# Relu and row sum on one core: a first load of 15 rows at a 60 KB pitch and a second of one row per partition

## The chip, the core and the metric

The kernel runs on one core of a Trainium2 chip. The metric is the device time in microseconds (us) of one execution; the kernel before takes 160.94 us, the median of three runs (160.9 to 161.1). The profile shows one further execution of it, taken by the hardware profiler, with a span of 159.6 us from its first instruction to its last.

## What is computed

`x` has 32 x 512 rows of 1024 float32 numbers, 64 MiB in all. Negative numbers count as zero, and each row is summed:

```python
def reference(x):
    relu_x = np.maximum(x, 0)
    return np.sum(relu_x, axis=-1).astype(np.float32)   # 16384 sums
```

So 67.1 MB are read once from HBM and 64 KB are written.

## The kernel before

**Tiling.** The 16384 rows are dealt to 128 partitions, 128 rows to each. A row is 4 KB. The first load brings rows 0 to 2047: partition p gets 16 consecutive rows, so that partitions lie 64 KB apart in HBM (`xf`, the pitch is 64 KB) and the whole load is one stretch of 8 MB. All later loads read from the other 14336 rows (`xv`), of which partition p owns 112 consecutive ones, so that the pitch is 448 KB; each full load takes 16 rows (64 KB) of every partition. There are seven full loads of 8 MB (`NB`, the list `TWO` has an entry for each), then a tail: a load of 8 rows, one of 4, and the last four rows of each partition in four loads of 9312, 5136, 960 and 976 bytes a partition. Full loads go around three buffers (`NBUF = 3`).

**Order.** Everything is written out by hand, with semaphores. SP issues every load and store, in program order, on one queue. The first load is moved ahead of the opening barrier (`EARLY = 1`). Loads 0 to 2 are issued at once. Load j from 3 on waits (in `load`, line 99) until DVE has finished with the buffer of load j - 3 (`freed`). The stores come last in SP's program (`store`, lines 109 and 110): the 16 sums of the first load, then 110 sums per partition, then the last two. The last instruction waits for all stores.

**Work on a load.** For most rows ACT clamps a group of rows in place (`clamp`, line 117) and DVE sums the group along the row (`total`, line 125). `TWO` gives the groups: `[16]` for loads 0 to 2, then `[8, 8]`, `[8, 8]`, `[7, 7]`. Single rows are done by one engine alone, clamp and sum in one instruction: `act_row` (line 132) on ACT, `dve_row` (line 140) on DVE. The seventh load, the tail and the last pieces are done in this way. The final sum, of the piece of 244 columns and three part sums, is line 224 on DVE.

Of the kernel before, what the change touches and what calls it, by code (L numbers as in the profile page):

```python
# [4 lines left out]
F32 = mybir.dt.float32  # L5
RELU = mybir.ActivationFunctionType.Relu
MAX, ADD = mybir.AluOpType.max, mybir.AluOpType.add
P = 128

ROWS = 16  # L10
NBUF = 3


TWO = [[16], [16], [16], [8, 8], [8, 8], [7, 7], []]
ACT = [0, 0, 0, 0, 0, 2, 9]
DVE = [0, 0, 0, 0, 0, 0, 7]

# [2 lines left out]
TAIL = [8, 4]  # L20
START_PIECE, END_PIECE = 280, 260
PIECES = [240, 244]
# [4 lines left out]
def kernel(tc: tile.TileContext, x: bass.AP, out: bass.AP):  # L27
    nc = tc.nc
    sems = Semaphores(tc)

    tc.close()
    tc.compile()
    nc.cur_bb = nc.bb_map[tc.start_bb_name]
    body = nc.cur_bb.bb.instructions
    ends = list(body)
    body.clear()
    n_stores = relu_sum(nc, sems, x, out)
    body.extend(ends)


    nc.cur_bb = nc.bb_map[tc.start_bb_name + "_end"]
    nc.cur_bb.bb.instructions.clear()
    nums = sorted(s.num for s in (*sems.loads, sems.act, sems.dve))
    cleared = range(nums[0], nums[-1] + 1)
    assert len(cleared) == len(nums)
    nc.sync.sem_clear(cleared)
    nc.sync.wait_ge(sems.stored, 16 * n_stores).then_inc(sems.stored, -16 * n_stores)
    open_without_barrier(tc, EARLY)


class Semaphores:
    def __init__(self, tc: tile.TileContext):
        n = len(TWO) + len(TAIL) + 2 + len(PIECES)
        self.loads = [tc.alloc_semaphore(f"load{i}") for i in range(n)]
        self.act = tc.alloc_semaphore("act")
        self.dve = tc.alloc_semaphore("dve")
        self.stored = tc.alloc_semaphore("stored")


def relu_sum(nc, sems: Semaphores, x: bass.AP, out: bass.AP):  # L60
    x_flat = x.flatten_outer_dims()
    N, D = x_flat.shape
    NT = N // P
    NB = len(TWO)
    assert N == P * NT == P * ROWS * (NB + 1)
# [3 lines left out]
    res = nc.alloc_sbuf_tensor("res", [P, NT], F32)  # L69
# [5 lines left out]
    ]  # L75


    N1 = P * ROWS
    xf = x_flat[:N1].rearrange("(p m) d -> p m d", p=P)
    xv = x_flat[N1:].rearrange("(p m) d -> p m d", p=P)  # L80
    o_flat = out.rearrange("b s -> (b s)")
    of = o_flat[:N1].rearrange("(p m) -> p m", p=P)
    ov = o_flat[N1:].rearrange("(p m) -> p m", p=P)

    def rows(m, n):
        if m < ROWS:
            return xf[:, m : m + n, :]
        return xv[:, m - ROWS : m - ROWS + n, :]

    def sums(m, n):  # L90
        if m < ROWS:
            return of[:, m : m + n], res[:, m : m + n]
        return ov[:, m - ROWS : m - ROWS + n], res[:, m : m + n]

    n_load = n_act = n_dve = n_store = 0
# [1 line left out]
    def load(dst, src, after=None):  # L97
        nonlocal n_load
        dma = nc.sync.dma_start(out=dst, in_=src)  # L99
        if after:  # L100
            dma.wait_op(sems.dve, after[1], "sem-ge")
        dma.then_inc(sems.loads[n_load], 16)
        n_load += 1
        return sems.loads[n_load - 1]

    def store(m, n, act, dve):
        nonlocal n_store
        dst, src = sums(m, n)
        nc.sync.wait_ge(sems.act, act)
        nc.sync.dma_start(out=dst, in_=src).wait_op(sems.dve, dve, "sem-ge").then_inc(  # L110
            sems.stored, 16
        )
        n_store += 1

    def clamp(ap, loaded):
        nonlocal n_act
        i = nc.scalar.activation(out=ap, in_=ap, func=RELU)  # L117
        if loaded is not None:
            i.wait_op(loaded, 16, "sem-ge")
        i.then_inc(sems.act, 1)  # L120
        n_act += 1

    def total(ap, m, n):
        nonlocal n_dve
        nc.vector.tensor_reduce(  # L125
            out=res[:, m : m + n], in_=ap, axis=mybir.AxisListType.X, op=ADD
        ).wait_op(sems.act, n_act, "sem-ge").then_inc(sems.dve, 1)
        n_dve += 1

    def act_row(ap, accum_out, loaded):  # L130
        nonlocal n_act
        i = nc.scalar.activation(out=ap, in_=ap, func=RELU, accum_out=accum_out)  # L132
        if loaded is not None:
            i.wait_op(loaded, 16, "sem-ge")
        i.then_inc(sems.act, 1)
        n_act += 1

    def dve_row(ap, accum_out, loaded):
        nonlocal n_dve
        i = nc.vector.tensor_scalar(  # L140
            out=ap,
            in0=ap,
            scalar1=0.0,
            scalar2=None,
            op0=MAX,
            op1=ADD,
            accum_out=accum_out,
        )
        if loaded is not None:
            i.wait_op(loaded, 16, "sem-ge")  # L150
        i.then_inc(sems.dve, 1)
        n_dve += 1

    freed = []
    m = 0
    for j in range(NB):
        buf = bufs[j % NBUF]
        loaded = load(buf[:, :, :], rows(m, ROWS), j >= NBUF and freed[j - NBUF])
        c = 0
        act_waits = dve_waits = loaded  # L160
        for n in TWO[j]:
            clamp(buf[:, c : c + n, :], act_waits)
            total(buf[:, c : c + n, :], m + c, n)
            act_waits = None
            c += n
        for _ in range(ACT[j]):
            act_row(buf[:, c, :], res[:, m + c : m + c + 1], act_waits)
            act_waits = None
            c += 1
        for _ in range(DVE[j]):  # L170
            dve_row(buf[:, c, :], res[:, m + c : m + c + 1], dve_waits)
            dve_waits = None
            c += 1
        assert c == ROWS
        freed.append((n_act, n_dve))
        m += ROWS


    buf = bufs[NB % NBUF]
    c = 0  # L180
    for n in TAIL:
        loaded = load(
            buf[:, c : c + n, :], rows(m, n), None if c else freed[NB - NBUF]
        )
        for i in range(n):
            if i % 2 == 0 or (n == 8 and i == 7):
                act_row(buf[:, c, :], res[:, m : m + 1], loaded if i == 0 else None)
            else:
                dve_row(buf[:, c, :], res[:, m : m + 1], loaded if i == 1 else None)
            c += 1  # L190
            m += 1

    flat = buf[:, :, :].rearrange("p c d -> p (c d)")
    src = rows(m, 4).rearrange("p c d -> p (c d)")
    at = c * D
    split = 2 * D
    b = split + START_PIECE
# [3 lines left out]
    loaded = load(flat[:, at : at + b], src[:, :b])  # L201
# [5 lines left out]
    loaded = load(flat[:, at + end : at + 4 * D], src[:, end:])  # L207
# [7 lines left out]

    store(0, ROWS, *freed[0])
    store(ROWS, NT - ROWS - 2, sums_act, sums_dve)

    for i in range(len(PIECES) - 1):
# [10 lines left out]
    ).wait_op(sems.dve, n_dve, "sem-ge").then_inc(sems.dve, 1)  # L232
    n_dve += 1
    store(NT - 2, 2, n_act, n_dve)
    return n_store

# [48 lines left out]
```

## Time and profile before

| what | value |
|---|---|
| time, median of 3 runs | 160.94 us (160.9 to 161.1) |
| span of the profiled execution | 159.6 us |
| difference, which lies around the span | 1.3 us |
| DVE busy | 117.6 us, 74% |
| ACT busy | 104.2 us, 65% |
| DMA queue, share of 16 engines | 98.0% |
| HBM read, mean rate over the span | 67.11 MB, 421 GB/s |
| instructions | 120 |

The page gives the profiled execution's own time as its span alone, 159.6 us; the runs' times are 1.3 us above it. Starts of instructions are counted from the start of the span. A DMA's own movement is no instruction: what is listed for SP is the issue, some 0.33 to 0.46 us each, and the landing comes later. The trace also records every DMA packet, one for each partition of a load or store, with start, duration and size.

### The profile page before, as it was taken

The numbers are of one execution on the slowest core, as the hardware profiler recorded it, in microseconds if no ns is written. First come the engines' busy times: TensorE is split into PE (matmuls) and PEld (weight loads), VectorE is DVE, ScalarE is ACT, GpSimd is POOL, SyncE is SP. The second block draws the span as 40 slices with busy tenths as digits, with TensorE's granted clock in tenths as the row PEclk, the third lists the DMA queues.
The fourth block names the chain that finished last, engine by engine and source line by source line (L and its number), as shares of the span: only waits on it lengthen the run. The fifth ranks groups of instructions, "written<-read, shape, count | busy, mean of one in ns | idle before, by whom it ended". The sixth has DMA issues, their size and how long they took to land.

```text
span 159.6 us, 120 instructions
## 1 busy us (share of the span) xinstructions
DVE 117.6 (74%) x43; ACT 104.2 (65%) x50; POOL 0.2 (0%) x4
## 2 busy tenths in 40 slices
DVE  0000000009999499994999999999999999999986
ACT  3000059990699708996099951999329993499995
POOL 0000000000000000000000000000000000000000
DMA  7996996996997999979979969969969969798993
GB/s 279 509 526 263 526 526 263 526 509 279 526 476 312 526 394 394 526 345 443 526 328 460 526 263 526 526 263 526 509 279 526 493 296 526 337 452 382 418 412 119
DMA packets 2304, 67.18 MB, mean 421 GB/s; under 512 B 640, under 2 KB 896, under 8 KB 1024
## 3 DMA queue, kind: packets, MB, share of 16 engines
q1 hardware_dynamic: 2304, 67.18, 98.0%
HBM read 67.11 MB, written 0.07 MB: 421 GB/s over the span
## 4 chain that ended last, share of the span: by engine, by line
DMA 43%; DVE 34%; ACT 17%; another core or an unknown queue 3%; SPq 1%; issue 0%
DMA io<-in_x_dram 43%; DVE res L125 32%; ACT io L117 17%; DVE io L140 1%; SPq L99 1%; DVE piece L224 0%; DVE piece L140 0%
## 5 line engine op out<-in xcount | busy, mean ns | idle before, releaser
L125 DVE TENSOR_REDUCE res<-io 128x8 f32<-128x8192 f32 (+2 forms) x9 | 101.1, 11287 | 40.0 <-ACT io L117 40.0
L117 ACT ACTIVATE io<-io 128x8192 f32<-128x8192 f32 (+2 forms) x9 | 81.7, 9110 | 47.7 <-DMA io<-in_x_dram 47.7
L132 ACT ACTIVATE io<-io 128x1024 f32<-128x1024 f32 x20 | 20.9, 1045 | 6.0 <-DMA io<-in_x_dram 6.0
L140 DVE TENSOR_SCALAR_CACHE_REDUCE io<-io 128x1024 f32<-128x1024 f32 (+2 forms) x15 | 15.8, 1110 | 0.5 <-DMA io<-in_x_dram 0.4
L132 ACT ACTIVATION_READ_ACCUMULATOR io<-io 128x1 f32 x20 | 3.8, 188 | 0.0
L117 ACT ACT_TABLE_LOAD x1 | 1.3, 1283 | 0.1
L140 DVE DVE_READ_ACCUMULATOR io<-io 128x1 f32 x15 | 1.2, 82 | 0.0
L224 DVE TENSOR_SCALAR_CACHE_REDUCE piece<-piece 128x247 f32<-128x247 f32 x1 | 0.4, 410 | 0.0
L140 DVE TENSOR_SCALAR_CACHE_REDUCE piece<-piece 128x240 f32<-128x240 f32 x1 | 0.4, 397 | 0.0
L269 POOL MEMSET const-bfloat16-1.0<- 128x1 bf16 x1 | 0.1, 101 | 0.0
L269 POOL MEMSET const-uint8-127<- 128x1 uint8 x1 | 0.1, 101 | 0.0
L269 POOL MEMSET const-float32-0.0<- 128x1 f32 x1 | 0.1, 98 | 0.2 <-issue 0.2
L269 POOL MEMSET const-float32-1.0<- 128x1 f32 x1 | 0.1, 98 | 0.0
L224 DVE DVE_READ_ACCUMULATOR piece<-piece 128x1 f32 x1 | 0.1, 83 | 0.0
L140 DVE DVE_READ_ACCUMULATOR piece<-piece 128x1 f32 x1 | 0.1, 82 | 0.0
## 6 DMA issues: line engine op xcount, KB each, us to landing
io<-in_x_dram SPq DMA_DIRECT2D x1, 4096.0 KB, 21.6
io<-in_x_dram SPq DMA_DIRECT2D x1, 2048.0 KB, 26.1
io<-in_x_dram SPq DMA_DIRECT2D x1, 1164.0 KB, 28.4
io<-in_x_dram SPq DMA_DIRECT2D x1, 642.0 KB, 29.5
piece<-in_x_dram SPq DMA_DIRECT2D x1, 122.0 KB, 29.2
piece<-in_x_dram SPq DMA_DIRECT2D x1, 120.0 KB, 29.4
io<-in_x_dram SPq DMA_DIRECT2D x7, 26.9
out_dram<-res SPq DMA_DIRECT2D x1, 55.0 KB, 1.6
```

The lines of the kernel that those rows point to most:

```text
L99: dma = nc.sync.dma_start(out=dst, in_=src)
L117: i = nc.scalar.activation(out=ap, in_=ap, func=RELU)
L125: nc.vector.tensor_reduce(out=res[:, m : m + n], in_=ap, axis=mybir.AxisListType.X, op=ADD).wait_op(sems.act, n_act, "sem-ge").then_inc(se ...
L132: i = nc.scalar.activation(out=ap, in_=ap, func=RELU, accum_out=accum_out)
L140: i = nc.vector.tensor_scalar(out=ap, in0=ap, scalar1=0.0, scalar2=None, op0=MAX, op1=ADD, accum_out=accum_out,)
L224: nc.vector.tensor_scalar(out=last[:, :], in0=last[:, :], scalar1=0.0, scalar2=None, op0=MAX, op1=ADD, accum_out=res[:, NT - 2 : NT - 1],) ...
L269: nc = _bacc.Bacc("TRN2", target_bir_lowering=False, num_devices=1)
```

## The change

The first load takes 15 rows for each partition, from rows 128 to 2047, so that partitions lie 60 KB apart. A second load brings rows 0 to 127, one stretch of 512 KB, one row (4 KB) for each partition, into the place left free in the same buffer. Only the first of the two stands ahead of the opening barrier. The single row of each partition is clamped and summed by DVE (`dve_row`) into a column of a new tile `one`, which DVE clears first and then transposes in blocks of 32 x 32 into `turned`; four partitions of `turned` then hold the 128 sums as 32 numbers each. The store of the first load's sums becomes three: the 15 sums (60 bytes) of the even partitions, those of the odd ones, and four stretches of 128 bytes from `turned`. The other two stores are as they were.

```diff
-TWO = [[16], [16], [16], [8, 8], [8, 8], [7, 7], []]
+TWO = [[15], [16], [16], [8, 8], [8, 8], [7, 7], []]
...
+    one = nc.alloc_sbuf_tensor("one", [P, 32], F32)
+    turned = nc.alloc_sbuf_tensor("turned", [P, 32], F32)
     N1 = P * ROWS
-    xf = x_flat[:N1].rearrange("(p m) d -> p m d", p=P)
+    xf = x_flat[P:N1].rearrange("(p m) d -> p m d", p=P)
...
-    of = o_flat[:N1].rearrange("(p m) -> p m", p=P)
+    oo = o_flat[:P].rearrange("(b i) -> b i", i=32)
+    of = o_flat[P:N1].rearrange("(p m) -> p m", p=P)
...
-        loaded = load(buf[:, :, :], rows(m, ROWS), j >= NBUF and freed[j - NBUF])
-        c = 0
+        c = 1 if j == 0 else 0
+        loaded = load(
+            buf[:, c:, :], rows(m + c, ROWS - c), j >= NBUF and freed[j - NBUF]
+        )
+        if j == 0:
+            ahead = load(buf[:, 0, :], x_flat[:P])
+        if j == 0:
+            nc.vector.memset(one[:, :], 0.0).then_inc(sems.dve, 1)
+            n_dve += 1
+            nc.vector.wait_ge(sems.dve, n_dve)
+            dve_row(buf[:, 0, :], one[:, 0:1], ahead)
+            nc.vector.transpose(turned[:, :], one[:, :]).wait_op(
+                sems.dve, n_dve, "sem-ge"
+            ).then_inc(sems.dve, 1)
+            n_dve += 1
+            sums_ahead = n_act, n_dve
...
-    store(0, ROWS, *freed[0])
+    store(1, ROWS - 1, *freed[0], slice(0, P, 2))
+    store(1, ROWS - 1, *freed[0], slice(1, P, 2))
+    store(0, 1, *sums_ahead)
     store(ROWS, NT - ROWS - 2, sums_act, sums_dve)
```

More of the change, by code (lines that the diff above doesn't have):

```diff
@@ L52, in __init__ @@
     def __init__(self, tc: tile.TileContext):
-        n = len(TWO) + len(TAIL) + 2 + len(PIECES)
+        n = 1 + len(TWO) + len(TAIL) + 2 + len(PIECES)
         self.loads = [tc.alloc_semaphore(f"load{i}") for i in range(n)]
@@ L86, in rows, with sums @@
         if m < ROWS:
-            return xf[:, m : m + n, :]
+            return xf[:, m - 1 : m - 1 + n, :]
         return xv[:, m - ROWS : m - ROWS + n, :]
-    def sums(m, n):
+    def sums(m, n, part):
         if m < ROWS:
-            return of[:, m : m + n], res[:, m : m + n]
+            return of[part, m - 1 : m - 1 + n], res[part, m : m + n]
         return ov[:, m - ROWS : m - ROWS + n], res[:, m : m + n]
@@ L104, in load, with store @@
         return sems.loads[n_load - 1]
-    def store(m, n, act, dve):
+    def store(m, n, act, dve, part=slice(None)):
         nonlocal n_store
-        dst, src = sums(m, n)
-        nc.sync.wait_ge(sems.act, act)
+        dst, src = (oo, turned[0::32, :]) if m == 0 else sums(m, n, part)
+        if act:
+            nc.sync.wait_ge(sems.act, act)
         nc.sync.dma_start(out=dst, in_=src).wait_op(sems.dve, dve, "sem-ge").then_inc(
```

## The prediction

> **What bounds the kernel.** I read the page's chain first, then the timeline, then busy time by stage, then the end. The chain:
>
> ```profile
> ## 4 chain that ended last, share of the span: by engine, by line
> DMA 43%; DVE 34%; ACT 17%; another core or an unknown queue 3%; SPq 1%; issue 0%
> ```
>
> It changes between engines, which hides what holds the pace. The timeline (start, duration, engine, line; in brackets the idle time before and what ended it) shows it:
>
> ```profile
> 21.87 13.86 ACT L117 ACTIVATE io<-io 128x16384 f32<-128x16384 f32 x1 [20.47 <-DMA io<-in_x_dram]
> ...
> 41.19 13.86 ACT L117 ACTIVATE io<-io 128x16384 f32<-128x16384 f32 x1 [5.46 <-DMA io<-in_x_dram]
> ...
> 60.55 13.86 ACT L117 ACTIVATE io<-io 128x16384 f32<-128x16384 f32 x1 [5.50 <-DMA io<-in_x_dram]
> 74.44 66.64 DVE L125 TENSOR_REDUCE res<-io 128x16 f32<-128x16384 f32 x7 [2.14 <-ACT io L117]
> 79.90 13.95 ACT L117 ACTIVATE io<-io 128x8192 f32<-128x8192 f32 x2 [5.50 <-DMA io<-in_x_dram]
> ```
>
> Each clamp starts as its load lands: 21.87, 41.19, 60.55, 79.90, that is 19.35 us apart, while ACT needs 13.9 and DVE 17.2. Loads set the pace. From 74.44 DVE works without a gap, through the seven totals and into the tail, but that run starts with the third load's clamp, so it moves with the loads. By stage (us, then DVE, ACT, POOL, clock, DMA share, GB/s):
>
> ```profile
> 41.20:60.50 19.30, 17.20 (x2) 13.85 (x1) 0.00 (x0) 1.00 1.00 435
> 60.50:79.90 19.40, 17.26 (x2) 13.86 (x1) 0.00 (x0) 1.00 1.00 432
> ```
>
> The DMA engines are full. The end, from the timeline:
>
> ```profile
> 155.37 1.22 DVE L140 TENSOR_SCALAR_CACHE_REDUCE io<-io 128x1024 f32<-128x1024 f32 x1 [0.43 <-DMA io<-in_x_dram]
> ...
> 157.74 0.41 DVE L224 TENSOR_SCALAR_CACHE_REDUCE piece<-piece 128x247 f32<-128x247 f32 x1
> ```
>
> DVE waits 0.43 us for the 9312-byte load, then works to 158.16; the last store follows and the span ends at 159.6. So a shift of the load stream before the third load moves DVE's run, the tail and the end alike, one for one, in both directions.
>
> **Where the stream loses time.** Only at its start. The first load needs 21.87 us where a load in the stream needs 19.35: 2.52 us. By the packet records the first packet starts 1.01 after the issue, the last packet of the load ends at 21.50, and its semaphore is complete at 21.85. What is left is 2.52 - 1.01 - 0.37 = 1.14 us: the ramp. The 16 engines' first packets start from 1.01 to 1.81, and last 2.50 to 3.27 us where all later 64 KB packets of this load last 2.418. The mean excess is 0.6, and by packet end less 2.418 the slowest engine is in step only at 2.17 (= 1.01 + 1.14, give or take 0.02). Its lag stays to the end: landings of a load are spread over 0.56 to 0.59 us throughout, and a load counts as landed with its slowest engine.
>
> **The change part by part.**
>
> *Packets.* Bytes stay the same; each engine gets 8 packets of 60 KB and 8 of 4 KB for 8 of 64 KB. Durations by size are 1.213 us (32 KB), 0.612 (16 KB), 0.199 (5136 B), 0.011 (64 B): a line with 0.0113 us for a packet. Eight more: +0.09 us. One more semaphore write of 0.009: +0.01. All of it is in the stream, on the path.
>
> *Issues.* Each load issued into the running stream (at 53.0, 72.3, 91.7, 108.9) stretched the packets in flight from 2.418 to about 2.43: 0.011. Six issues between 126.9 and 129.3 stretched theirs to 2.474, about 0.01 each. The change issues one load and two stores more: +0.03. Before any gain that is +0.13 us.
>
> [...]
>
> *The ramp.* What the new pitch does to it no row shows. Lower end: it goes to nothing, -1.14. If only the excess goes and the engines' starts stay, the slowest is in step at its start, 1.81 for 2.17: -0.36. For a shorter spread of starts speaks the last store, whose 16 engines begin within some 0.04 us (159.01 to 159.04). Upper end: a longer ramp, priced below. At 64 KB pitch the engines' first addresses are whole multiples of 64 KB apart and all read the same offset at once; at 60 KB these offsets differ. I take -0.57, half of the ramp, between the two rows: the excess is a thing of simultaneous starts (the engine starting at 1.81 has 0.08 of it, the one at 1.05 has 0.85), and the spread should shrink partly with it. Sum: -0.57 + 0.13 = -0.44 us.
>
> [...]
>
> *First buffer.* ACT clamps 15 rows in 15/16 of 13.86 = 13.0 us, from about 20.6 (without a gain) to 33.6, and DVE totals them in 16.1 to 49.7, where it was 52.98. The fourth load is then issued 3.2 us earlier, behind a queue filled to 60.2: worth nothing. Before this DVE has a memset, a row (1.21 + 0.08) and a transpose (no row; 0 to 0.41, the 247-column instruction) at about 22 to 24, queued ahead of the first total, which waits for ACT until 33.6: hidden by some 10 us; uncovered they would cost 1.8 us.
>
> *Stores.* The two added issues (0.36 us each) stand in SP's program behind the last load, at about 129.3, and SP has nothing to do until 156.5: hidden. Their packets queue behind the pieces. Before, eight 64 B packets an engine ended at 157.18 and the 110-sum store began at 157.46; eight of 60 B, one more semaphore, and on four engines a 128 B packet with one more, cost 0.01 to 0.04 by the 64 B row and 0.14 by the 440 B row (0.0257 each): under the 0.28 of cover, and the last store comes only at 159.0. Store traffic stretched some 976 B packets from 0.045 to 0.051-0.061; the last piece landed at 157.60 and DVE came to it at 157.72, cover 0.1. I take zero, and up to +0.05.
>
> **The rivals.**
>
> *The ramp has nothing to do with the pitch.* A cold path that any first packet meets gives no gain, and the sum is +0.13: 161.07 us. For it: later packets of engines that start within 2 ns of each other (4.276, 4.278, 4.282) last 2.418, at the same 64 KB multiples. Against: an engine's excess depends on who else starts.
>
> *The ramp is moved.* Engines that leave the second load in step meet the same multiples at the 448 KB pitch and pay there: also about 161.07. Against: the 448 KB load follows from the first one now without one slow packet.
>
> *Slower: the ramp is made by issues.* Three loads are issued in the first 1.33 us, and their descriptors fall into the ramp; the change puts a fourth among them. A third of 1.14 is +0.38, with 0.13 +0.51: 161.45 us. It decides from +0.19 us on, where the sum passes +0.32. For it: the ramp ends about when the third load's issue, 0.9 to 1.33, has had 1.0 us to reach the engines. Against: six issues in a row near 128 cost 0.055 together. A 4 KB phase slower than the line (0.20 us a packet for 0.16) would cost about as much.
>
> **How the numbers follow.** The time is the median plus the change of the span: 160.94 - 0.44 = 160.50. A measurement of this kernel can tell about 0.2%, 0.32 us. A shorter ramp: 0.55, from 159.93 (-1.14 + 0.13) to 160.94; 0.46 of it beyond 0.32, which asks for a ramp shorter by 0.45, and 0.09 within. Ramp independent of the pitch: 0.13; moved: 0.07; both within. Longer: 0.25, slower. The rest of uncertainty of this kind I put at 0.02, from within to slower. So 0.46, 0.27, 0.27. The range leaves out the last tenth on each side: 160.05 to 161.40; the likeliest case's own is 160.05 to 160.75.
>
> **What would show it.** Right: first packets of 60 KB near 2.27 us and starts within less than 0.8 us; the first clamp at about 20.1 (eight packets shorter by 0.15, and the 0.57); the second at 41.19 + 0.11 - 0.57 = 40.73, all later ones 0.46 earlier; 4 KB packets at 0.16; DVE's run from 73.98. Wrong: a second clamp at 41.3 (no gain) or 41.6 (issues); slow packets in the first 448 KB load (moved); 4 KB packets over 0.18; or a tail in which DVE waits for the pieces.

## The result, and the profile after

The changed kernel takes 161.56 us, the median of five runs (161.52 to 161.60), beside 161.03 for the kernel before (160.90 to 161.16): a ratio of 1.0032, 95% interval 1.0021 to 1.0043. It is slower by 0.53 us, where 0.44 faster was forecast. The profiled execution has a span of 160.1 us, 0.49 more than before.

The chain of the changed kernel has the same links in nearly the same shares, so it does not tell where 0.5 us went:

```profile
## 4 chain that ended last, share of the span: by engine, by line
DMA 44%; DVE 33%; ACT 17%; another core or an unknown queue 3%; SPq 1%; issue 0%
```

Its timeline tells (start, duration, engine, line; in brackets the idle time before and what ended it):

```profile
21.04 13.00 ACT L121 ACTIVATE io<-io 128x15360 f32<-128x15360 f32 x1 [19.64 <-DMA io<-in_x_dram]
22.29 1.22 DVE L144 TENSOR_SCALAR_CACHE_REDUCE io<-io 128x1024 f32<-128x1024 f32 x1 [22.05 <-DMA io<-in_x_dram]
...
23.55 0.21 DVE L173 STREAM_TRANSPOSE turned<-one 128x32 f32<-128x32 f32 x1
34.07 16.15 DVE L129 TENSOR_REDUCE res<-io 128x15 f32<-128x15360 f32 x1 [10.31 <-ACT io L121]
41.64 13.86 ACT L121 ACTIVATE io<-io 128x16384 f32<-128x16384 f32 x1 [7.60 <-DMA io<-in_x_dram]
...
60.99 13.86 ACT L121 ACTIVATE io<-io 128x16384 f32<-128x16384 f32 x1 [5.50 <-DMA io<-in_x_dram]
74.88 66.65 DVE L129 TENSOR_REDUCE res<-io 128x16 f32<-128x16384 f32 x7 [2.13 <-ACT io L121]
```

The second clamp starts at 41.64, before at 41.19: 0.45 us are lost by then. After that nothing is lost: the third clamp is 0.44 late, DVE's long run 0.44. The added row, the transpose (0.21 us) and the total of 15 rows lie far ahead of their turn. By stage the stream is full as before (columns as in the prediction):

```profile
41.20:60.50 19.30, 14.00 (x2) 13.86 (x1) 0.00 (x0) 1.00 1.00 435
60.50:79.90 19.40, 17.27 (x2) 13.86 (x1) 0.00 (x0) 1.00 1.01 436
```

And the end, again from the timeline, is the same picture 0.44 to 0.48 us later:

```profile
155.81 1.22 DVE L144 TENSOR_SCALAR_CACHE_REDUCE io<-io 128x1024 f32<-128x1024 f32 x1 [0.44 <-DMA io<-in_x_dram]
...
158.22 0.41 DVE L244 TENSOR_SCALAR_CACHE_REDUCE piece<-piece 128x247 f32<-128x247 f32 x1
```

So the loss is in the start of the stream. The packet records split it. I call an engine "in step" at the end of its first packet less the duration that packets of this size have later (2.418 us for 64 KB, 2.268 for 60 KB). Before, the 16 engines are in step at 1.83 us on average, the slowest at 2.17; after, at 1.95 and 2.52. The slowest has lost 0.35. The rest of the 0.45 is 0.07 for packets (8 x (2.268 + 0.159) for 8 x 2.418) and small change. The engines also keep their distance from each other: landings of one load are spread over 0.56 to 0.59 us before and 0.87 to 0.89 us after, the second load as the eighth. The pitch was to bring the engines together at the start; it drove them apart.

### The profile page after: what moved, and what is told of

Its sections match the earlier page's. It is cut to its first block, busy times and chain, and to the rows that moved or that the text cites. A ratio compares the mean times of both kernels' runs of the same rounds, so it can differ in the third digit from the quotient of the medians.

```text
span 160.1 us, 129 instructions
## 1 busy us (share of the span) xinstructions
DVE 118.1 (74%) x47; ACT 103.4 (65%) x50; POOL 0.2 (0%) x4
## 4 chain that ended last, share of the span: by engine, by line
DMA 44%; DVE 33%; ACT 17%; another core or an unknown queue 3%; SPq 1%; issue 0%
DMA io<-in_x_dram 44%; DVE res L129 32%; ACT io L121 17%; SPq L102 1%; DVE io L144 0%; DVE piece L244 0%; DVE piece L144 0%
## 5 line engine op out<-in xcount | busy, mean ns | idle before, releaser
L129 DVE TENSOR_REDUCE res<-io 128x8 f32<-128x8192 f32 (+3 forms) x9 | 100.0, 11170 | 17.7 <-ACT io L121 17.7
L121 ACT ACTIVATE io<-io 128x8192 f32<-128x8192 f32 (+3 forms) x9 | 80.9, 9015 | 49.0 <-DMA io<-in_x_dram 49.0
L144 DVE TENSOR_SCALAR_CACHE_REDUCE io<-io 128x1024 f32<-128x1024 f32 (+2 forms) x16 | 17.1, 1121 | 22.6 <-DMA io<-in_x_dram 22.5
```

The costliest lines, as they stand in the source:

```text
L129: nc.vector.tensor_reduce(out=res[:, m : m + n], in_=ap, axis=mybir.AxisListType.X, op=ADD).wait_op(sems.act, n_act, "sem-ge").then_inc(se ...
L144: i = nc.vector.tensor_scalar(out=ap, in0=ap, scalar1=0.0, scalar2=None, op0=MAX, op1=ADD, accum_out=accum_out,)
```

## The experiments

Three theories stood after this. **Issues**, the slower rival of the prediction: a fourth DMA issued within the first 2 us lengthens the ramp. **Pitch**: reading at 60 KB itself puts the slowest engine later. A third was that the ramp is a cold path that neither touches. Each comparison has its own runs of the kernel before on its chip, with a median of 161.04 to 161.09 us.

**1. The split without the pitch.**

```diff
-TWO = [[16], ...
+TWO = [[15], ...
...
+        c = 1 if j == 0 else 0
+        loaded = load(buf[:, c:, :], rows(m + c, ROWS - c), ...)
+        if j == 0:
+            ahead = load(buf[:, 0:1, :], rows(0, 1))      # xf as before: pitch 64 KB
+            dve_row(buf[:, 0, :], res[:, 0:1], ahead)
```

> The kernel before with only its first load split at the old pitch of 64 KB: 15 rows per partition, then the one row left, which DVE clamps and sums; stores as before. So it has the fourth early issue without the new pitch and without the new stores. Theory of the issues (a fourth issue within the first 2 us makes the ramp longer): the ramp grows by about the 0.35 us that the slowest engine lost in the changed kernel, 0.09 for packets and semaphores, together +0.45 us, second clamp at about 41.6. Theory of the pitch (60 KB itself puts the slowest engine later): +0.1 us, second clamp at 41.3.

Measured: 161.22 beside 161.09, ratio 1.0008 (0.9999 to 1.0016), +0.13 us. Slowest engine in step at 2.25, landings of a full load spread over 0.52 to 0.57 us. The clamp of the first 448 KB load in this kernel:

```profile
41.42 13.86 ACT L117 ACTIVATE io<-io 128x16384 f32<-128x16384 f32 x1 [7.57 <-DMA io<-in_x_dram]
```

That is between the two expectations, 41.3 and 41.6, but the time agrees with the price of packets and issue alone (+0.1), not with +0.45. A fourth early issue with packets of 60 KB does not make the loss: the interval, -0.02 to +0.26 us, holds the 0.1 and not the 0.45.

**2. The pitch without the fourth early issue.** The changed kernel with the single row loaded later, into a tile of its own.

```diff
-        if j == 0:
-            ahead = load(buf[:, 0, :], x_flat[:P])
+        if j == 2:
+            nc.sync.wait_ge(sems.act, 1)
+            ahead = load(alone[:, :], x_flat[:P])
...
```

> The changed kernel with its single-row load taken out of the start: issued only after the first clamp, into a tile of its own, summed by DVE between the second and the third total. The first load keeps 15 rows at 60 KB; three issues stand in the first 1.4 us as in the kernel before. Theory of the issues: the slowest engine is in step at about 2.17 us as before, what is left is packets and stores, +0.1 to +0.15 us against the kernel before. Theory of the pitch: the slowest engine is in step at about 2.5 us, +0.45 to +0.5 us.

Measured: 161.39 beside 161.09, ratio 1.0017 (1.0008 to 1.0026), +0.30 us; slowest engine in step at 2.44. The ramp is that of the theory of the pitch (2.5 expected) though only three loads are issued early; the time is below its +0.45.

**3. The kernel before with one issue in the ramp.**

```diff
+    nc.vector.memset(bufs[2][:, 0:8, :], 0.0).then_inc(sems.dve, 1)
+    n_dve += 1
...
+        if j == 1:
+            nc.sync.wait_ge(sems.dve, 1)
```

> The kernel before, with loads 1 and 2 issued only when a DVE memset of a free buffer is over (some us after the start, still long before the first load has landed). One issue is left in the ramp. Theory of the issues: each of the three costs about 0.35 us of the ramp of 1.14, so two fewer give -0.7 us, and first packets start closer together than 0.8 us and last less than 2.6. Theory of the pitch, and that of a cold path: 0, first packets as before, slowest engine in step at 2.17.

Measured: 161.09 beside 161.09, ratio 0.9997 (0.9989 to 1.0006). Loads 1 and 2 were issued at 8.77 and 9.14 us, the memset being over at 8.73:

```profile
1.85 6.88 DVE L156 MEMSET io<- 128x8192 f32 x1 [1.85 <-issue]
21.88 13.86 ACT L117 ACTIVATE io<-io 128x16384 f32<-128x16384 f32 x1 [20.48 <-DMA io<-in_x_dram]
```

The first clamp starts at 21.88 all the same (21.87 before), and the slowest engine is in step at 2.18. At 64 KB the ramp does not depend on the issues behind it: -0.7 was expected of the theory of the issues, 0 came.

**4. The changed kernel with one issue in the ramp**, the same edit in the changed kernel, ahead of its second load.

> The changed kernel with the same delay ahead of its second load: 60 KB pitch, one issue in the ramp. Theory of the issues: ramp as in the delayed kernel before, so about -0.7 from the ramp, +0.1 for packets, +0.05 for the tail: -0.55 us against the kernel before. Theory of the pitch: as the changed kernel, +0.5. A cold path: the ramp of before, +0.15.

Measured: 161.50 beside 161.09, ratio 1.0019 (1.0011 to 1.0028); slowest engine in step at 2.42. Again no gain of the kind that issues would give. Whether 0.41 is less than the 0.53 of the changed kernel, this run can't say, since the two were not measured side by side; in numbers 13 and 14 they are.

**5 to 8. The pitch alone.** One number changed in the kernel before, nothing else: same instructions, same packets of 64 KB, same stores.

```diff
-    xf = x_flat[:N1].rearrange("(p m) d -> p m d", p=P)
+    xf = bass.AP(x_flat.tensor, x_flat.offset, [[PITCH * D, P], [D, ROWS], [1, D]])
```

> The kernel before with one number changed: the first load still takes 16 rows (64 KB) of every partition in one DMA, but from addresses 60 KB apart, so that one row in 16 is read twice and the sums of the first load are of other rows than the reference's. No split, no new instruction, stores as before. Theory of the pitch: 60 KB alone makes the engines leave the ramp further apart, landings spread over 0.85 to 1.0 us instead of 0.56, the slowest in step at 2.42 to 2.52 instead of 2.17, +0.25 to +0.35 us. Rival (the split or the smaller packet does it, the split load at 64 KB was a lucky one): spread 0.56, time within 0.1 us of the kernel before.

> As the kernel with the 60 KB pitch alone, but at 68 KB (17 rows): again the sums of the first load are of other rows. If any pitch that is no multiple of 64 KB spreads the engines, this gives +0.25 to +0.35 us too, with landings 0.85 to 1.0 us apart; if 60 KB is special, or the partitions' overlap in reads is what matters (none here), it gives the time of the kernel before.

> As above at 512 KB (128 rows), a multiple of 64 KB and a large power of two; the sums of the first load are of other rows. If multiples of 64 KB are what keeps the engines together: spread 0.5 to 0.6 us, time within 0.1 us of the kernel before. [...]

> As above at 32 KB (8 rows, so that neighbouring partitions read half of their rows twice; the sums of the first load are of other rows). Half of the partitions are multiples of 64 KB apart. Theory of the multiples of 64 KB: between the two, spread 0.6 to 0.85 us, +0.1 to +0.2 us; if it is a matter of smaller pitches than 64 KB: as the 60 KB one or worse.

Measured: 60 KB 161.37 (ratio 1.0016, 1.0007 to 1.0025), 68 KB 161.62 (1.0035, 1.0021 to 1.0048), 512 KB 161.43 (1.0026, 1.0016 to 1.0037), 32 KB 161.00 (0.9997, 0.9988 to 1.0006), all beside 161.09. Here are the first two clamps at 60 KB, then at 68 KB:

```profile
22.08 13.86 ACT L118 ACTIVATE io<-io 128x16384 f32<-128x16384 f32 x1 [20.67 <-DMA io<-in_x_dram]
41.42 13.86 ACT L118 ACTIVATE io<-io 128x16384 f32<-128x16384 f32 x1 [5.49 <-DMA io<-in_x_dram]
```

```profile
22.47 13.86 ACT L118 ACTIVATE io<-io 128x16384 f32<-128x16384 f32 x1 [21.07 <-DMA io<-in_x_dram]
41.79 13.86 ACT L118 ACTIVATE io<-io 128x16384 f32<-128x16384 f32 x1 [5.46 <-DMA io<-in_x_dram]
```

The first clamp comes 0.21 and 0.60 us later than before, the second 0.23 and 0.60: what is lost in the first packets stays lost, nothing is added. The pitch alone does it, in one DMA, without a split. That 512 KB costs about as much, and 32 KB nothing, was not what the theory of multiples of 64 KB expected. The Trainium skill's page "DMA: Bandwidth & Descriptors", section "Latency and other measured facts", has 207 GB/s per direction at a row pitch of 512 KiB, for copies between HBM tensors in tiles of 128 partitions x 16 KiB, and calls 214 the full rate; by that row 512 KiB costs next to nothing. This case agrees: with 64 KB per partition the median packet of the 512 KB load lasts 2.420 us, at 64 KB 2.418, and only the ramp is longer.

**9 and 10. The stores.** The changed kernel again, and without its three early stores.

```diff
-    store(1, ROWS - 1, *freed[0], slice(0, P, 2))
-    store(1, ROWS - 1, *freed[0], slice(1, P, 2))
-    store(0, 1, *sums_ahead)
```

> The changed kernel unchanged, beside the next one on the same chip. If pitch and split are all there is: +0.39 us (0.26 of the 60 KB pitch alone and 0.13 of the split alone), slowest engine in step at 2.4 to 2.5. If the fourth early issue or the stores add something: about +0.53 as first measured.

> The changed kernel without its three early stores (the sums of rows 0 to 2047 are not written). If the stores cost nothing on the path, as forecast: the time of the changed kernel to within 0.05 us. If three early stores for one cost the 0.05 to 0.14 us that the parts leave over: the changed kernel less about 0.1.

Measured: 161.59 and 161.59 beside 161.04, ratios 1.0032 (1.0020 to 1.0045) and 1.0031 (1.0019 to 1.0042). No cost of the stores shows; with intervals of some 0.2 us to each side, 0.1 us would not show. The changed kernel's loss repeats, +0.55.

**11 and 12. More pitches**, the one-number edit again.

> The kernel before with the first load's addresses 16 KB apart (4 rows; neighbouring partitions read three quarters of their rows twice, and the sums of the first load are of other rows). If it matters that the first packets of the engines lie at multiples of 64 KB from each other (an engine has 8 partitions, so that 16 engines' first partitions lie at least 4 apart): landings spread 0.5 to 0.6 us, time as the kernel before within 0.1 us. If the smaller pitch or the smaller stretch of memory shortens the ramp: -0.1 to -0.4 us.

> The same at 128 KB (32 rows; the sums of the first load are of other rows). If multiples of 64 KB keep the engines together and 512 KB is a case of its own: time of the kernel before within 0.1 us, spread 0.5 to 0.6. If the stretch of memory is what spreads them (8 MB at 64 KB, 16 MB here, 64 MB at 512 KB, where +0.42 was measured): +0.1 to +0.3 us, engines starting later as at 512 KB.

Measured beside 161.04: 16 KB 161.38 (ratio 1.0020, 1.0011 to 1.0029), 128 KB 161.01 (0.9998, 0.9989 to 1.0007). The expectation that 16 KB would cost nothing missed; so did the one that a longer stretch of memory is what counts.

**13 and 14. What is left over.** The changed kernel and its delayed form on one chip.

> The changed kernel once more, beside its delayed form on the same chip. Pitch alone gave +0.26 us and the split alone +0.13; the changed kernel gave +0.53 and +0.55. If the fourth issue within the ramp costs something at this pitch: +0.5 us here, and 0.1 to 0.15 less in the delayed form; the fourth issue lasts 0.77 us or more here. If the rest was chance between chips: both +0.4 us.

> The changed kernel with all loads but the first issued some 9 us after the start, again. Issues in the ramp cost something at 60 KB: +0.4 us, slowest engine in step at 2.4; they cost nothing: the changed kernel's time.

Measured: 161.49 and 161.44 beside 161.06, ratios 1.0030 (1.0019 to 1.0042) and 1.0029 (1.0018 to 1.0040). The second clamps, of the changed kernel and of the delayed one:

```profile
41.52 13.86 ACT L121 ACTIVATE io<-io 128x16384 f32<-128x16384 f32 x1 [7.59 <-DMA io<-in_x_dram]
```

```profile
41.57 13.86 ACT L121 ACTIVATE io<-io 128x16384 f32<-128x16384 f32 x1 [7.59 <-DMA io<-in_x_dram]
```

No gain shows from taking the issues out of the ramp, at this pitch either: the two differ by 0.05 us. So the theory of the issues has fallen as the cause at both pitches. A share of 0.1 us at 60 KB is not excluded, since the intervals are some 0.18 us to each side. The fourth issue itself lasted 0.72 to 0.86 us in the undelayed changed kernels, 0.52 in the split at 64 KB and 0.47 to 0.48 delayed, with nobody waiting for it.

**15 and 16. A rule for the pitch?**

> The kernel before with the first load's addresses 96 KB apart (24 rows; the sums of the first load are of other rows). 32, 64 and 128 KB kept the time of the kernel before, 60 and 68 KB did not. If multiples of 32 KB are what does it: within 0.1 us of the kernel before, spread 0.4 to 0.6. If powers of two are: +0.25 to +0.55, spread 0.8 to 1.2.

> The same at 132 KB (33 rows; the sums of the first load are of other rows), 4 KB off the pitch of 128 KB, which cost nothing. If being 4 KB off a multiple of 32 KB is what spreads the engines, as at 60 and 68 KB: +0.25 to +0.55 us, spread 0.8 to 1.2. If it was a matter of 8 MB stretches only: within 0.1 us of the kernel before.

Measured beside 161.06: 96 KB 161.16 (ratio 1.0015, 1.0004 to 1.0026; single runs from 161.03 to 161.90), 132 KB 160.96 (0.9995, 0.9987 to 1.0004). Being 4 KB off a good pitch does not cost at 128 KB. So neither multiples of 32 or 64 KB, nor powers of two, nor the stretch of memory explain the nine pitches: 32, 64, 128 and 132 KB are alike, 96 KB is a little worse at most, 16, 60, 68 and 512 KB cost 0.28 to 0.53 us. Why stays open. Each pitch alone was measured on one chip, 32, 60, 68 and 512 KB on the same, 16 and 128 KB on a second, 96 and 132 KB on a third, so a part of the chip in this pattern is not excluded. The trace names no engine for a packet, so which engine is late, and on which addresses, can't be read from it.

One view joins them. Taken from the profiled execution of each, in us:

| kernel | slowest engine in step | span | span less slowest |
|---|---|---|---|
| before | 2.17 | 159.62 | 157.45 |
| before, two issues delayed | 2.18 | 159.68 | 157.50 |
| pitch 16 KB | 2.49 | 159.94 | 157.45 |
| pitch 32 KB | 2.18 | 159.65 | 157.47 |
| pitch 128 KB | 2.05 | 159.63 | 157.58 |
| pitch 96 KB | 2.33 | 159.82 | 157.50 |
| pitch 132 KB | 2.31 | 159.84 | 157.53 |
| pitch 60 KB | 2.40 | 159.84 | 157.44 |
| pitch 68 KB | 2.79 | 160.26 | 157.47 |
| pitch 512 KB | 2.58 | 160.04 | 157.46 |
| split at 64 KB | 2.25 | 159.91 | 157.66 |
| pitch 60 KB, late row | 2.44 | 160.04 | 157.60 |
| changed | 2.52 | 160.11 | 157.59 |
| changed, again | 2.77 | 160.32 | 157.55 |
| changed, a third time | 2.42 | 159.97 | 157.55 |
| changed, fewer stores | 2.68 | 160.24 | 157.57 |
| changed, delayed | 2.42 | 160.01 | 157.59 |
| changed, delayed, again | 2.44 | 160.04 | 157.60 |

The last column is 157.44 to 157.58 for all that have eight packets of 64 KB an engine in the first load, and 157.55 to 157.66 for those with the split: in these kernels whatever moved the slowest engine's first packet moved the end one for one, and the split adds its 0.1. The first column varies between executions of one kernel too (2.42 to 2.77 for the changed one), so one profile places a kernel only roughly; the timed runs decide. At 132 KB, for one, the profiled execution took 161.19 us, where the median is 160.96.

## Why the prediction was wrong, and where it was right

*The step that failed is the ramp*, the term of -0.57. The slowest engine's ramp grew by 0.35 in the profile after. With the pitch alone, the time rose by 0.28 where that term foresaw a fall of 0.57. No row of the trace before showed what the pitch does, and the prediction said so; it then let an argument choose the sign (same offsets read at once must collide, different ones should not). The runs at 32, 64 and 128 KB, where the ramp is short, and at 60 and 68 KB, where it is long, are against that argument; at 132 KB the offsets differ too, and the time did not fall clear of its interval. A row that the prediction had under its first rival spoke against it as well: three second packets started at the same multiples of 64 KB without a stretch. They start within 6 ns (4.276, 4.278, 4.282), not within the 2 ns that stand there.

*Mean and slowest.* The prediction worked with the slowest engine, which was right: the average in-step time rose by 0.12 only, the slowest one's by 0.35, and the table shows that the slowest one sets the end.

*The sum without the ramp fits.* +0.13 was worked out for packets, semaphores and issues; the split alone gave +0.13, if with an interval from -0.02 to +0.26, and without the two added stores. Packets came at 2.268 and 0.159 us, where 2.27 and 0.16 were foreseen.

*The covers held.* DVE's row and transpose ended at 23.76, ahead of the 34.07 of the first total; the fourth load was issued at 50.25 for 53.00 and nothing came of it; the early stores show no cost (numbers 9 and 10).

*The rivals.* The slower one had the size, 161.45 for 161.56, but by luck: its mechanism was wrong, as numbers 1, 3, 13 and 14 show that issues don't make the ramp. Its sign, a second clamp at 41.6, came too (41.64), and did not tell one cause of a longer ramp from another. A ramp that does not depend on the pitch is excluded by numbers 5 to 7 and 11, where one number alone made it longer. "The ramp is moved" is excluded by the packets of the first 448 KB load, none of which lasts longer than 2.418. The range, 160.05 to 161.40, took the issues' price as the upper end of the ramp and ended 0.16 short; 0.09 of this is the kernel before, with a median of 160.94 in three runs and 161.03 beside the changed one.

*What stays open*: why the engines come apart at some pitches, and a remainder. Pitch alone (+0.28) and split alone (+0.13) make 0.41, while six comparisons of the changed kernel, its delayed form and the form with fewer stores among them, give 0.38 to 0.55. The intervals, 0.13 to 0.2 us to each side, allow the sum; they don't prove it.

No version here beats the kernel before beyond its interval; the nearest, 132 KB alone, reads other rows than the reference's and is 0.9987 to 1.0004 of it.

## What to carry to other kernels

Here, where a full load stream holds the kernel from the first packet to the last, the lag of the slowest DMA engine after its first packet was paid in full at the end (the last column of the table). So look in such a kernel at the first packets of all engines, and at the slowest rather than the mean. Four of the nine pitches of the first load cost 0.28 to 0.53 us here, none gained clear of its interval, and no simple rule in the pitch was found: try the pitch by itself, as one number, before building a split, a transpose and new stores around it. Where the trace shows nothing of a term, its sign is open too, and the sum without it is the better middle.

## What was not expected of the hardware

The 16 engines did not make up for their start: the spread of a load's landings, 0.56 us at the second load, is still 0.56 at the eighth, 97 us later, and 0.87 in the changed kernel; only at 68 KB does it shrink a little, from 1.19 to 1.12. A first load at a 512 KB pitch ran its later packets at full pace (2.420 us at the median for 64 KB) and lost 0.34 us in all, at the start. In its profiled execution the pitch of 132 KB had the lowest mean in-step time of all, 1.71 us, and gained nothing by it, since one engine was in step only at 2.31.
